# Token factors of a pre-norm applied after the projection, a first norm with its weights as columns, and small parameters loaded inside the feed-forward

## The chip, the cores and the metric

The kernel runs on 1 core of one Trainium2 chip. The metric is the device time of one launch in microseconds. Three runs of the kernel before gave 1834.03, 1839.99 and 1847.09 us, so the median is 1839.99 us.

## The reference, cut to what matters

Ten sublayers work on 256 tokens of 1024 features. Layers 0 and 1 each have a SwiGLU feed-forward (hidden 2816), a mixer (retention and gated delta heads), cross attention to a memory, and a second feed-forward. A last block has another mixer (called mix2 here) and an MLP with squared ReLU (hidden 4096). All values are float32. Each sublayer sits between two RMS norms:

```
h = sublayer(rms_norm(x, w_pre));  x = x + f * rms_norm(h, w_post)     # f = 0.5 or 1
rms_norm(x, w) = x * rsqrt(mean(x*x) + 1e-6) * w
swiglu(u) = (silu(u @ Wg) * (u @ Wu)) @ Wd
mlp(u)    = square(relu(u @ W1)) @ W2
```

The factor rsqrt(mean(x*x) + 1e-6) is one number for each token. It commutes with a projection: (r*u) @ W = r*(u @ W).

## The kernel before, in words

The 256 tokens are two tiles of 128 (t = 0, 1). The residual x stands in SBUF, tokens on partitions. For a projection the normed input u is transposed on PE (L439), 128x128 at a time, into a PSUM tile `tr`, and split into a rounded part and a rest: ACT casts `xh` (L393), DVE subtracts to get `xl` (L394). Each weight arrives as a raw unit of 128x1024 (512 KB) through the SP queue (L410), and is split in the same way into `wh` (ACT, L393) and `wl` (DVE, L394; every second unit of the first mixers' input projection on POOL). A product is then three matmuls (`mm3`, L430): wh with xh, wh with xl, wl with xh. There are 3 raw buffers and 8 pairs of wh and wl; the weights are fetched ahead in the order of their use.

`normT` (L483) is the norm before a sublayer: two squares with sums on ACT (L488), then on POOL an addition (L490), a multiply-add (L453) and a power (L456), then on DVE two `u` (L495), and after each `u` four transposes and the split. `post` (L498) is the norm after it: two squares of the PSUM banks on ACT (L502), the same three steps on POOL (L504, L453, L456), then on DVE `pd` (L510) twice, which needs the factor, and the additions to x (L512). Feed-forward blocks (`ffn`, L600) run over six pieces of the hidden width, j = 0 to 5. In the last piece token tile 0 is finished first, and its `post` and next `normT` run while PE does the down projection of tile 1; then tile 1 follows.

The order of the instructions on every engine comes from the framework's scheduler, which places them by a simulated timeline; engines take them strictly in that order. `gate` (L323) orders a DMA behind the last matmul of a product that was recorded before it (`anchor`), without a wait on the chip. A DMA that is not gated may be placed as early as its buffers allow: small parameters of both layers' mixers (`wab`, `alog`, `dtb`, `lgam`, `gdn_norm`, `conv`, L778 to L789), the `positions` (L662) and mix2's vector of parameters (`pv`, L1291) stand at the start of the SP queue.

Of the kernel before, what the change touches and what calls it, by code (L numbers as in the profile page):

```python
# [108 lines left out]
def pack(inputs):  # L109

    g = {k: np.asarray(v) for k, v in inputs.items()}
    a = {k: g[k] for k in ("norm_pre", "norm_post", "mem_norm", "gdn_norm")}
    a["x"], a["mem"] = g["x"][0], g["mem"][0]
# [156 lines left out]
class K:  # L270
    marks = None

    def __init__(self, ctx, tc, A, out):
# [14 lines left out]
        self.tables, self.used = self.cst.tile([128, 5744], F32, name="tables"), 0  # L288
# [194 lines left out]
    def normT(self, src, wb, T, t):  # L483
# [3 lines left out]
        for g in range(2):  # L487
            nc.scalar.activation(self.junk, src[:, g * 512:g * 512 + 512], AF.Square, accum_out=ss[:, g:g + 1])  # L488
        s1 = self.small(1, "s1")
        nc.gpsimd.tensor_tensor(out=s1, in0=ss[:, 0:1], in1=ss[:, 1:2], op=ALU.add)  # L490
        rs = self.rsqrt(s1, 1.0 / DM, EPS)
        for g in range(2):
            sl = slice(g * 512, g * 512 + 512)
            u = self.w("u")
            nc.vector.scalar_tensor_tensor(out=u, in0=src[:, sl], scalar=rs, in1=wb[:, sl], op0=ALU.mult, op1=ALU.mult)  # L495
            self.toT(u, T, g * 4, 4, t)

    def post(self, t, banks, wb, half):  # L498
        nc = self.nc
        ss = self.small(2, "ss2")  # L500
        for g in range(2):
            nc.scalar.activation(self.junk, banks[g], AF.Square, accum_out=ss[:, g:g + 1])  # L502
        s1 = self.small(1, "s1")
        nc.gpsimd.tensor_tensor(out=s1, in0=ss[:, 0:1], in1=ss[:, 1:2], op=ALU.add)  # L504
        f = 4.0 if half else 1.0
        rs = self.rsqrt(s1, f / DM, f * EPS)
        for g in range(2):
            d = self.w("pd")
            sl = slice(g * 512, g * 512 + 512)
# [90 lines left out]
    def ffn(self, l, s, T, wpost, after):  # L600
# [6 lines left out]
        def act(t, pg, pu, fw):  # L607
# [3 lines left out]
            nc.scalar.activation(s_[:, :fw], pg[:, :fw], AF.Silu)  # L611
# [1416 lines left out]
```

## Time and profile before

| | |
|---|---|
| median of 3 runs | 1839.99 us |
| the profiled execution's own time | 1836.08 us |
| its span | 1834.0 us |
| PE busy | 1768.2 us (96%) |
| DVE, ACT, POOL busy | 1077.6, 908.2, 201.9 us |
| mean granted TensorE clock | 0.975 |
| instructions | 25097 |

The page gives busy time by engine, 40 slices of the span, the DMA queues, the chain that ended last and the costliest groups. In a timeline row the first two numbers are start and duration in us; what stands in square brackets is the idle time of that engine just before the row, and who ended it. "x2" means two instructions merged into a row. A granted clock of 1.00 is 2.4 GHz, 0.50 is 1.2 GHz.

### The profile page before, as it was taken

Reading aid. Unit: us, or ns where it says so; the run is one execution under the profiler, and the core shown is the slowest. Engines: PE = TensorE matmul, PEld = TensorE weight load, DVE = VectorE, ACT = ScalarE, POOL = GpSimd, SP = SyncE. Lnnn points to the kernel's source line nnn. Section 1 sums busy time; section 2 is a strip of 40 time slices with the busy share of each in tenths; the row PEclk is TensorE's granted clock in tenths of the full one; section 3 lists DMA queues with packets and bytes.
Section 4 is the critical chain, followed back from the end, with each engine's and each line's share of the span. In section 5 each row is a group of like instructions: output and inputs, shape, how many; then the busy total and the mean of one; then the engine's idle time right before and its main releaser. Section 6 shows DMA issues by size and latency. Waiting matters only on the chain. (4 is left out here: it accounts for less than half of the span.)

```text
span 1834.0 us, 25097 instructions
## 1 busy us (share of the span) xinstructions
PE 1768.2 (96%) x9712; PEld 1517.9 (83%) x9712; DVE 1077.6 (59%) x1544; ACT 908.2 (50%) x1458; POOL 201.9 (11%) x240
## 2 busy tenths in 40 slices
PE   7999999999999999999999999999999899989998
PEld 6888799888988887888789988988888788878886
DVE  5454577765555546555467676546455668465554
ACT  5434565545544445444465464545344676344442
POOL 0000343121000000000133211000000120110000
PEclk9999999999999999999999999999999999599999
DMA  7555432434536664656544332636567532135552
GB/s 250 207 200 198 155 130 76 132 96 146 162 137 197 197 197 143 207 185 202 187 144 138 96 115 84 206 122 205 164 196 219 170 135 76 39 126 173 187 177 84
DMA packets 82775, 287.05 MB, mean 157 GB/s; under 512 B 11104, under 2 KB 12512, under 8 KB 82656
## 3 DMA queue, kind: packets, MB, share of 16 engines
q1 hardware_dynamic: 82656, 285.46, 47.9%
q8 instruction: 76, 1.25, 0.3%
q14 instruction: 43, 0.35, 0.1%
HBM read 284.37 MB, written 1.05 MB: 156 GB/s over the span
## 5 line engine op out<-in xcount | busy, mean ns | idle before, releaser
L394 DVE TENSOR_TENSOR wl<-raw,wh 128x1024 fp32r<-128x1024 f32 x473 | 576.6, 1231 | 361.3 <-ACT wh L393 323.6
L393 ACT CAST wh<-raw 128x1024 fp32r<-128x1024 f32 x505 | 521.1, 1051 | 339.8 <-DMA raw<-in_wst 196.3
L436 PE MATMUL mm<-wh,xh 128*128 128x512 f32 (+1 forms) x1184 | 457.7, 388 | 6.4 <-ACT xh L393 6.1
L436 PE MATMUL mm<-wh,xl 128*128 128x512 f32 (+1 forms) x1184 | 452.5, 385 | 8.7 <-DVE xl L394 8.6
L436 PE MATMUL mm<-wl,xh 128*128 128x512 f32 (+1 forms) x1184 | 453.1, 384 | 0.3 <-DVE wl L394 0.3
L436 PEld LDWEIGHTS mm<-wh,xl 128*128 128x128 f32 x1184 | 225.2, 191 | 55.0 <-DVE xl L394 12.8
L436 PEld LDWEIGHTS mm<-wh,xh 128*128 128x128 f32 x1184 | 226.0, 191 | 51.2 <-ACT xh L393 10.2
L436 PEld LDWEIGHTS mm<-wl,xh 128*128 128x128 f32 x1184 | 225.7, 191 | 41.3 <-DVE wl L394 1.1
L436 PE MATMUL bank<-wh,xh 128*128 128x512 f32 x544 | 213.3, 392 | 4.4 <-ACT xh L393 4.4
L436 PE MATMUL bank<-wl,xh 128*128 128x512 f32 x544 | 213.8, 393 | 0.0
L436 PE MATMUL bank<-wh,xl 128*128 128x512 f32 x544 | 201.7, 390 | 0.0
L436 PE MATMUL mm<-xh,wh 128*128 128x256 f32 x552 | 160.1, 290 | 0.0
L436 PE MATMUL mm<-xh,wl 128*128 128x256 f32 x552 | 158.5, 288 | 0.7 <-DVE wl L394 0.6
L436 PE MATMUL mm<-xl,wh 128*128 128x256 f32 x552 | 158.7, 288 | 0.0
L394 DVE TENSOR_TENSOR xl<-tr,xh 128x512 fp32r<-128x512 f32 (+1 forms) x118 | 77.2, 664 | 108.0 <-ACT xh L393 107.8
L394 POOL TENSOR_TENSOR wl<-raw,wh 128x1024 fp32r<-128x1024 f32 x32 | 84.7, 2649 | 458.5 <-ACT wh L393 451.9
L393 ACT CAST xh<-tr 128x512 fp32r<-128x512 f32 (+1 forms) x118 | 65.9, 565 | 135.3 <-PE tr L439 134.4
L436 PEld LDWEIGHTS bank<-wh,xh 128*128 128x128 f32 x544 | 102.1, 188 | 28.0 <-ACT xh L393 6.4
L436 PEld LDWEIGHTS bank<-wh,xl 128*128 128x128 f32 x544 | 102.2, 188 | 21.1
L436 PEld LDWEIGHTS bank<-wl,xh 128*128 128x128 f32 x544 | 102.2, 188 | 20.5
L436 PEld LDWEIGHTS mm<-xh,wl 128*128 128x128 f32 x552 | 106.7, 194 | 2.2 <-DVE wl L394 1.5
L436 PEld LDWEIGHTS mm<-xh,wh 128*128 128x128 f32 x552 | 106.9, 194 | 1.4 <-issue 0.7
(458 smaller groups left out, 2004.5 us busy)
## 6 DMA issues: line engine op xcount, KB each, us to landing
raw<-in_wst SPq DMA_DIRECT2D x505, 512.0 KB, 4.4
wpre<-in_norm_pre SPq DMA_DIRECT2D x8, 512.0 KB, 6.5
wpost<-in_norm_post SPq DMA_DIRECT2D x8, 512.0 KB, 6.1
mem<-in_mem SPq DMA_DIRECT2D x4, 512.0 KB, 3.4
rel<-in_rel SPq DMA_DIRECT2D x2, 512.0 KB, 4.4
wmem<-in_mem_norm SPq DMA_DIRECT2D x2, 512.0 KB, 3.8
out<-tables SPq DMA_DIRECT2D x4, 256.0 KB, 2.1
abias<-in_abias SPq DMA_DIRECT2D x3, 256.0 KB, 4.1
```

The lines of the kernel that those rows point to most:

```text
L393: a = self.nc.scalar.copy(h, raw)
L394: return a, (eng or self.nc.vector).tensor_tensor(out=l, in0=raw, in1=h.bitcast(F32), op=ALU.subtract)
L436: return self.place(self.nc.tensor.matmul(out, a, b, start=start, stop=stop))
```

## The change

Three things. (1) Five of the ten pre-norms become "late" (both feed-forwards of both layers, and the MLP; the very first of them in its own form): `u` is x times the weights, without the token factor, and the factor goes into the activation after the projection, as a scale operand of Silu and a factor of the product with `up`, or squared in front of the ReLU. The very first norm transposes x itself, and multiplies by the weights (now a column, `gain0`, 128x8) while it splits; the 512 KB broadcast of that norm's weights is not loaded any more. (2) All norms: the mean's factor goes into the squares' scale, and POOL has two steps in place of three. In `post`, `pd` is bank times weights and needs no factor; the addition to x applies it. (3) The mixer's small parameters are loaded and prepared in piece 3 of the feed-forward before it (`mixer_params`), and `positions`, `madd`, `pv`, `rst` and `lrubd` are gated.

```diff
+    def first_norm(self, T, t, late):
+        for g in range(2):
+            ps = self.tbank()
+            self.transposes(ps, self.x[t][:, g * 512:g * 512 + 512], 4)
+            sl, gn = slice(t * 128, (t + 1) * 128), lambda i: self.gain0[:, g * 4 + i:g * 4 + i + 1]
+            for i in range(4):
+                self.nc.scalar.activation(T[0][g][:, i, sl], ps[:, i * 128:i * 128 + 128], AF.Copy, scale=gn(i))
+            for i in range(4):
+                self.nc.vector.scalar_tensor_tensor(out=T[1][g][:, i, sl], in0=ps[:, i * 128:i * 128 + 128], scalar=gn(i),
+                                                    in1=T[0][g][:, i, sl].bitcast(F32), op0=ALU.mult, op1=ALU.subtract)
+        self.mean_rsqrt([self.x[t][:, g * 512:g * 512 + 512] for g in range(2)], 1.0, late)
...
-    def normT(self, src, wb, T, t):
+    def mean_rsqrt(self, halves, f, out=None, then=None):
         nc = self.nc
         ss = self.small(2, "ss")
         for g in range(2):
-            nc.scalar.activation(self.junk, src[:, g * 512:g * 512 + 512], AF.Square, accum_out=ss[:, g:g + 1])
+            nc.scalar.activation(self.junk, halves[g], AF.Square, scale=math.sqrt(f / DM), accum_out=ss[:, g:g + 1])
+            if then:
+                then(g)
         s1 = self.small(1, "s1")
-        nc.gpsimd.tensor_tensor(out=s1, in0=ss[:, 0:1], in1=ss[:, 1:2], op=ALU.add)
-        rs = self.rsqrt(s1, 1.0 / DM, EPS)
+        nc.gpsimd.tensor_scalar(out=s1, in0=ss[:, 1:2], scalar1=ss[:, 0:1], scalar2=f * EPS, op0=ALU.add, op1=ALU.add)
+        r = self.small(1, "rs") if out is None else out
+        nc.gpsimd.tensor_tensor(out=r, in0=s1, in1=self.mhalf, op=ALU.pow)
+        return r
+
+    def normT(self, src, wb, T, t, late=None):
...
+            if late is None:
+                nc.vector.scalar_tensor_tensor(out=u, in0=halves[g], scalar=rs, in1=w, op0=ALU.mult, op1=ALU.mult)
+            else:
+                nc.vector.tensor_tensor(out=u, in0=halves[g], in1=w, op=ALU.mult)
             self.toT(u, T, g * 4, 4, t)
+        if late is not None:
+            self.mean_rsqrt(halves, 1.0, late)
...
+        def then(g):
+            d = self.w("pd")
+            nc.vector.tensor_tensor(out=d, in0=banks[g], in1=wb[:, g * 512:g * 512 + 512], op=ALU.mult)
+            ds.append(d)
+        rs = self.mean_rsqrt(banks, 4.0 if half else 1.0, None, then)
         for g in range(2):
...
-            nc.vector.scalar_tensor_tensor(out=d, in0=banks[g], scalar=rs, in1=wb[:, sl], op0=ALU.mult, op1=ALU.mult)
-            xg = self.x[t][:, sl]
-            nc.vector.tensor_tensor(out=xg, in0=xg, in1=d, op=ALU.add)
+            xg = self.x[t][:, g * 512:g * 512 + 512]
+            nc.vector.scalar_tensor_tensor(out=xg, in0=ds[g], scalar=rs, in1=xg, op0=ALU.mult, op1=ALU.add)
...
-            nc.scalar.activation(s_[:, :fw], pg[:, :fw], AF.Silu)
+            nc.scalar.activation(s_[:, :fw], pg[:, :fw], AF.Silu, scale=rs[t])
             h = self.w("hf")
-            nc.vector.tensor_tensor(out=h[:, :fw], in0=pu[:, :fw], in1=s_[:, :fw], op=ALU.mult)
+            nc.vector.scalar_tensor_tensor(out=h[:, :fw], in0=pu[:, :fw], scalar=rs[t], in1=s_[:, :fw], op0=ALU.mult, op1=ALU.mult)
...
+            if j == TBJ and s == 1:
+                self.mixer_params(l)
...
+    def mixer_params(self, l):
+        nc, A = self.nc, self.A
+        wab = self.small(128, "wab")
+        self.gate(nc.sync.dma_start(wab, A["wab"][l]))
+        wabh, wabl = self.rtile[:, :128], self.rtile[:, 128:256]
+        self.split(wab, wabh, wabl)
...
+        nc.scalar.activation(nega, par[:, 8:16], AF.Exp)
...
-        nc.sync.dma_start(self.pv, A["pv"])
+        self.gate(nc.sync.dma_start(self.pv, A["pv"]))
...
+                if j == 0:
+                    nc.vector.tensor_tensor(out=r2[t], in0=rs[t], in1=rs[t], op=ALU.mult)
                 r_ = self.w("relu")
-                nc.scalar.activation(r_, ps, AF.Relu)
+                nc.scalar.activation(r_, ps, AF.Relu, scale=r2[t])
...
+        late = lambda l, s: (l, s) == (2, 1) or l < 2 and s in (0, 3)
         self.fetch()
         nc.sync.dma_start(self.x[1], A["x"][128:])
...
-            self.normT(self.x[t], wp, T, t)
+            self.first_norm(T, t, rs[t])
```

How the order moves, at three places. First the SP queue at the start of the program (every row is a DMA; `raw` is a weight unit, `tables` the SBUF tile that holds x, the identity and the small parameters). Before:

```order
L1969 DMA tables<-in_x 128x512 x2
L387 DMA wpre<-in_norm_pre 128x1024
L341 DMA tables<-in_ident 128x128
L410 DMA raw<-in_wst 128x1024
L1974 DMA tables<-in_x 128x1024
L410 DMA raw<-in_wst 128x1024 x2
L662 DMA tables<-in_positions 128x2
L786 DMA tables<-in_gdn_norm 128x1
L778 DMA wab<-in_wab 128x128
L783 DMA tables<-in_alog 128x8
L786 DMA tables<-in_gdn_norm 128x1
L1291 DMA tables<-in_pv 128x33
```

And now:

```order
L2007 DMA tables<-in_x 128x512
L342 DMA tables<-in_ident 128x128
L2010 DMA tables<-in_x 128x512
L342 DMA tables<-in_gain 128x8
L411 DMA raw<-in_wst 128x1024
L2013 DMA tables<-in_x 128x1024
L411 DMA raw<-in_wst 128x1024 x36
L1980 DMA madd_890<-in_madd 128x256
L692 DMA tables<-in_positions 128x2
L342 DMA tables<-in_invf 128x64
L811 DMA tables<-in_gdn_norm 128x1
L803 DMA wab<-in_wab 128x128
```

Before, fourteen small loads stood around the fourth weight unit; now none stands among the first 37 units. In layer 1 six small loads follow one another in the same piece of its feed-forward, and eleven loads in place of eight stand in front of mix2.

Second the ACT queue at the start (`sg` is the Silu of the first gate, the two `xh` after it in the rows of before are those of token tile 1). Before:

```order
L393 CAST wh<-raw 128x1024 x2
L393 CAST rtile<-wab 128x128
L861 ACTIVATE tables<-tables 128x8 x2
L393 CAST wh<-raw 128x1024
L611 ACT_TABLE_LOAD
L611 ACTIVATE sg<-mm 128x256
L393 CAST wh<-raw 128x1024
L393 CAST xh<-tr 128x4x128 x2
```

And now, from the first weight on (`xh` of tile 0's second half, then squares and `xh` of tile 1):

```order
L394 CAST wh<-raw 128x1024
L472 ACTIVATE xh<-tr,tables 128x128 x4
L502 ACTIVATE tables,ss<-tables 128x512
L472 ACTIVATE xh<-tr,tables 128x128 x4
L502 ACTIVATE tables,ss<-tables 128x512
L394 CAST wh<-raw 128x1024 x3
L472 ACTIVATE xh<-tr,tables 128x128 x4
L639 ACT_TABLE_LOAD
L639 ACTIVATE sg<-mm,tables 128x256
```

The last `xh` of tile 1 moved from behind the fifth weight's cast to behind the fourth's. Five activation table loads are new, all of them inside the first feed-forward of layer 0 (three) and of layer 1 (two), around the Exp of `mixer_params` and the sines of the rotary tables.

Third the DVE queue between layer 0's second feed-forward and layer 1's first (a late pre-norm). Before:

```order
L613 TENSOR_TENSOR hf<-mm,sg 128x512
L394 TENSOR_TENSOR wl<-raw,wh 128x1024 x2
L394 TENSOR_TENSOR xl<-tr,xh 128x4x128
L510 SCALAR_TENSOR_TENSOR pd<-bank,rs_6384,wpost 128x512 x2
L512 TENSOR_TENSOR tables<-tables,pd 128x512 x2
L495 SCALAR_TENSOR_TENSOR u<-tables,rs_6403,wpre 128x512 x2
L510 SCALAR_TENSOR_TENSOR pd<-bank,rs_6454,wpost 128x512 x2
L394 TENSOR_TENSOR xl<-tr,xh 128x4x128 x2
L512 TENSOR_TENSOR tables<-tables,pd 128x512 x2
L495 SCALAR_TENSOR_TENSOR u<-tables,rs_6469,wpre 128x512 x2
```

And now:

```order
L641 SCALAR_TENSOR_TENSOR hf<-mm,tables,sg 128x512
L395 TENSOR_TENSOR wl<-raw,wh 128x1024 x2
L535 TENSOR_TENSOR pd<-bank,wpost 128x512 x2
L395 TENSOR_TENSOR xl<-tr,xh 128x4x128
L540 SCALAR_TENSOR_TENSOR tables<-pd,rs,tables 128x512 x2
L523 TENSOR_TENSOR u<-tables,wpre 128x512 x2
L535 TENSOR_TENSOR pd<-bank,wpost 128x512 x2
L395 TENSOR_TENSOR xl<-tr,xh 128x4x128
L540 SCALAR_TENSOR_TENSOR tables<-pd,rs,tables 128x512 x2
L395 TENSOR_TENSOR xl<-tr,xh 128x4x128
L523 TENSOR_TENSOR u<-tables,wpre 128x512 x2
```

`pd` reads no factor any more, the addition to x does (`rs`), and `u` reads none. On PE the transposes of `u` stand where they stood at most boundaries; at the two boundaries from cross attention to the second feed-forward they moved up among the matmuls of the output projection.

## Rows read from the trace of the kernel before

**Rows 1.** Page, part 1: busy us (share) and instructions of each engine.
```profile
PE 1768.2 (96%) x9712; PEld 1517.9 (83%) x9712; DVE 1077.6 (59%) x1544; ACT 908.2 (50%) x1458; POOL 201.9 (11%) x240
```
**Rows 2.** Waits of PE from 30 us on: total us, times, longest.
```profile
PE tr L439 <- DVE u L495: 11.0, 10, 1.9
PE mm L436 <- DVE xl L394: 8.6, 7, 1.6
...
PE mm L436 <- ACT xh L393: 2.6, 5, 1.2
...
PE mm L436 <- DVE wl L394: 0.8, 3, 0.3
```
**Rows 3.** Timeline of the first 24 us: start, duration, engine, instruction.
```profile
9.17 1.05 ACT L393 CAST wh<-raw 128x1024 fp32r<-128x1024 f32 x1 [4.09 <-DMA raw<-in_wst]
...
17.91 1.05 ACT L393 CAST wh<-raw 128x1024 fp32r<-128x1024 f32 x1 [3.21 <-DMA raw<-in_wst]
...
21.88 1.04 ACT L393 CAST wh<-raw 128x1024 fp32r<-128x1024 f32 x1 [1.23 <-DMA raw<-in_wst]
...
23.47 0.39 PE L436 MATMUL mm<-wh,xh 128*128 128x256 f32 x1 [3.52 <-ACT xh L393]
```
**Rows 4.** Timeline of SP: the fourth weight unit is issued.
```profile
13.85 0.43 SPq L410 DMA_DIRECT2D raw<-in_wst  x1
```
**Rows 5.** Stretches: us, busy time by engine, granted clock, DMA share, GB/s.
```profile
101.00:108.00 7.00, 7.00 (x32) 5.78 (x31) 1.79 (x3) 2.99 (x4) 0.00 (x0) 1.00 0.02 6
8.00:10.00 2.00, 1.18 (x6) 1.18 (x7) 1.43 (x3) 0.83 (x1) 0.00 (x0) 1.00 1.02 418
12.00:14.00 2.00, 1.98 (x10) 1.88 (x9) 1.29 (x3) 2.00 (x4) 0.94 (x3) 1.00 0.19 32
```
**Rows 6.** Timeline of PE at the first boundary, feed-forward to mixer.
```profile
207.99 1.38 PE L439 MATMUL tr<-tables,u 128*128 128x128 f32 x8 [0.54 <-DVE u L495]
...
211.65 0.50 PE L436 MATMUL mm<-wh,xl 128*128 128x512 f32 x1 [1.59 <-DVE xl L394]
```
**Rows 7.** Timeline of DVE, ACT and POOL at that boundary.
```profile
203.71 1.28 DVE L512 TENSOR_TENSOR tables<-tables,pd 128x512 f32<-128x512 f32 x2
...
206.32 0.19 POOL L453 TENSOR_SCALAR rs<-s 128x1 f32<-128x1 f32 x1
...
...
207.18 1.42 DVE L495 SCALAR_TENSOR_TENSOR u<-tables,rs,wpre 128x512 f32<-128x512 f32 x2 [2.19 <-POOL rs L456]
...
209.59 1.41 DVE L510 SCALAR_TENSOR_TENSOR pd<-bank,rs,wpost 128x512 f32<-128x512 f32 x2 [1.00 <-POOL rs L456]
...
209.89 2.94 ACT L393 CAST wh<-raw 128x1024 fp32r<-128x1024 f32 x3
...
210.92 1.28 DVE L394 TENSOR_TENSOR xl<-tr,xh 128x512 fp32r<-128x512 f32 x2
```
**Rows 8.** Stretches at half clock behind boundaries, first and last of three, columns as in rows 5.
```profile
212.30:215.70 3.40, 3.40 (x10) 2.62 (x9) 3.40 (x3) 1.25 (x3) 2.04 (x1) 0.50 0.00 0
...
1635.70:1642.50 6.80, 5.64 (x14) 4.17 (x14) 6.62 (x9) 4.28 (x8) 2.24 (x3) 0.50 0.20 54
```
**Rows 9.** Groups by line: form, count, busy us, mean ns, idle before.
```profile
L394 DVE TENSOR_TENSOR wl<-raw,wh 128x1024 fp32r<-128x1024 f32 x473 | 576.6, 1231 | 361.3 <-ACT wh L393 323.6
...
L613 DVE TENSOR_TENSOR hf<-mm,sg 128x512 f32<-128x512 f32 x40 | 27.3, 684 | 13.5 <-PE mm L436 13.5
...
L1143 DVE SCALAR_TENSOR_TENSOR y<-o,rs,zz 128x128 f32<-128x128 f32 x16 | 4.5, 346 | 0.0
```
**Rows 10.** One line, L611: count, duration ns min/median/max, first and last start.
```profile
L611 ACT ACTIVATE sg<-mm x48: 383/592/598, 20.3 to 1411.3; 128x512 f32<-128x512 f32 x40, 128x256 f32<-128x256 f32 x8
...
L611 ACT ACT_TABLE_LOAD x3: 1283/1283/1283, 19.0 to 1242.2; - x3
```
**Rows 11.** DMA issues: KB each, median us from issue to landing.
```profile
raw<-in_wst SPq DMA_DIRECT2D x505, 512.0 KB, 4.4
...
tables<-in_positions SPq DMA_DIRECT2D x1, 1.0 KB, 8.3
```

More of the change, by code (lines that the diff above doesn't have):

```diff
@@ L287, in __init__ @@
         nc = self.nc
-        self.tables, self.used = self.cst.tile([128, 5744], F32, name="tables"), 0
+        self.tables, self.used = self.cst.tile([128, 5776], F32, name="tables"), 0
         self.x = []
@@ L492, in normT @@
+        r = self.small(1, "rs") if out is None else out
+        nc.gpsimd.tensor_tensor(out=r, in0=s1, in1=self.mhalf, op=ALU.pow)
+        return r
+    def normT(self, src, wb, T, t, late=None):
+        nc = self.nc
+        halves = [src[:, g * 512:g * 512 + 512] for g in range(2)]
+        if late is None:
+            rs = self.mean_rsqrt(halves, 1.0)
         for g in range(2):
-            sl = slice(g * 512, g * 512 + 512)
+            w = wb[:, g * 512:g * 512 + 512]
             u = self.w("u")
-            nc.vector.scalar_tensor_tensor(out=u, in0=src[:, sl], scalar=rs, in1=wb[:, sl], op0=ALU.mult, op1=ALU.mult)
+            if late is None:
+                nc.vector.scalar_tensor_tensor(out=u, in0=halves[g], scalar=rs, in1=w, op0=ALU.mult, op1=ALU.mult)
+            else:
+                nc.vector.tensor_tensor(out=u, in0=halves[g], in1=w, op=ALU.mult)
@@ L661, in rotary_tables @@
         pi = self.tab(2).bitcast(I32)
-        nc.sync.dma_start(pi, A["positions"])
+        self.gate(nc.sync.dma_start(pi, A["positions"]))
         pf = self.small(2, "posf")
@@ L768, in mixer_plan @@
         self.plan(("w_out", l), 8)
+    def mixer_params(self, l):
[4 more added lines that the diff above has]
+        self.split(wab, wabh, wabl)
+        par = self.small(24, "par")
+        self.gate(nc.sync.dma_start(par[:, 0:8], self.bc(A["dtb"][l], 8)))
+        self.gate(nc.sync.dma_start(par[:, 8:16], self.bc(A["alog"][l], 8)))
+        self.gate(nc.sync.dma_start(par[:, 16:24], self.bc(A["lgam"][l], 8)))
+        nw = self.small(1, "gdnw")
+        self.gate(nc.sync.dma_start(nw, A["gdn_norm"][l].rearrange("(p o) -> p o", o=1)))
+        nc.vector.tensor_scalar(out=nw, in0=nw, scalar1=0.5, scalar2=None, op0=ALU.mult)
+        cw = self.small(60, "cw")
+        self.gate(nc.sync.dma_start(cw, A["conv"][l]))
+        nega = self.small(8, "nega")
+        nc.scalar.activation(nega, par[:, 8:16], AF.Exp)
+        nc.vector.tensor_scalar(out=nega, in0=nega, scalar1=-1.0, scalar2=None, op0=ALU.mult)
+        self.params = wabh, wabl, par, nw, cw, nega
     def mixer(self, l, T, wpost, after):
@@ L776, in mixer @@
         self.mark("ab")
[L777 to L790 removed]
+        wabh, wabl, par, nw, cw, nega = self.params
         self.st = "m"
@@ L1967, in run @@
         norm = lambda l, s, w: self.bcast(A[two[s, w]] if l == 2 else A["norm_" + w][l, s], "w" + w)
-        for g in range(2):
-            nc.sync.dma_start(self.x[0][:, g * 512:g * 512 + 512], A["x"][:128, g * 512:g * 512 + 512])
         self.anchor = None
+        nc.sync.dma_start(self.x[0][:, :512], A["x"][:128, :512])
         self.ident = self.const("ident", 128)
-        wp = norm(*subs[0], "pre")
+        self.gain0 = self.const("gain0", 8)
+        nc.sync.dma_start(self.x[0][:, 512:], A["x"][:128, 512:])
+        late = lambda l, s: (l, s) == (2, 1) or l < 2 and s in (0, 3)
         self.fetch()
@@ L2005, in run @@
             if l == 2:
-                (self.mix2 if s == 0 else self.mlp)(T, po, after)
+                if s == 0:
+                    self.mix2(T, po, after)
+                else:
+                    self.mlp(T, po, after, rs)
             elif s == 0 or s == 3:
-                self.ffn(l, 1 if s == 0 else 2, T, po, after)
+                self.ffn(l, 1 if s == 0 else 2, T, po, after, rs)
             elif s == 1:
```

47 lines of the change are left out of this document (13 added, 34 removed).

## The prediction, as it was put on record

> **What bounds the kernel now.** I read the page first. PE is busy for 1768.2 of 1834.0 us [rows 1], and no other engine comes near, so a change that adds no matmul can only win where PE stands still or runs at half clock. Then the waits of PE. In the first 24 us PE waits for its first data and then, once, 3.52 us for `xh` [rows 3]. From 30 us on, 11.0 us go to transposes that wait for `u`, ten times, 8.6 us to matmuls that wait for `xl`, 2.6 us to matmuls that wait for `xh`, and 0.8 us to `wl` [rows 2]. The first two lie at the boundaries between sublayers, and the last number says that the weights are in time once the start is over. What is left of PE's idle time belongs to the mixers' own chains, which the change leaves alone.
>
> Then one boundary, where the reader is to see a chain in series. PE stands 0.54 us before `u` and 1.59 us before `xl` [rows 6]. Before the first `u`, DVE adds to x, ACT squares, POOL takes its steps, and DVE has been idle for 2.19 us when the factor comes; the wait for `xl` is a matter of order on DVE: two `pd` of tile 1, which themselves waited 1.00 us for POOL, stand ahead of it from 209.59 us [rows 7]. Last the clock: behind this boundary PE has 3.40 us at a granted clock of 0.50 (1.2 GHz), and behind the last one 6.80 us; the third, between them in time, is like the first [rows 8].
>
> **The start.** Before, the first weight's cast starts at 9.17 us, when its transfer has landed [rows 3]. Now 512 KB less stand ahead of it (the weights' broadcast). At the 418 GB/s that the queue moved then [rows 5] that is 1.25 us, at the three quarters of it that a busy ramp may give 1.7; I take 1.4, so the cast starts at 7.8, ends at 8.85 (1.05 us, [rows 3]), and its `wl` ends at 10.1 (1.231 us of DVE, [rows 9]). That frees the first raw buffer, and the fourth unit is issued at 10.1 in place of 13.85 us [rows 4], because no small load stands ahead of it; DMA moved only 32 GB/s from 12 to 14 us [rows 5], so this was time lost on SP. With the median landing of 4.4 us [rows 11] it lands at 14.5 and not just before 17.91 [rows 3]. On ACT tile 1's last `xh` now stands behind this fourth cast, not behind the fifth, which began at 21.88 [rows 3]. So: cast to 15.5, four scaled copies of 128 columns to 16.7 (0.3 us each is an estimate, a little under the 0.346 us that DVE takes for as many columns, [rows 9]), the four `xl` on DVE at 0.346 us each overlapping to about 17.6. PE then goes on with tile 1 at 17.6 and not at 23.47: **6 us less**. The bounds: if the fourth unit lands as late as it did (17.91), 2.5 us; if the first weight lands as early as the queue's full rate lets it and the copies cost no more than one cast, 8.5.
>
> **The boundaries, waits for `u`.** Of the chain before `u`, each norm and each `post` loses one POOL step, 0.19 us [rows 7] and the gap to the next, by estimate 0.27 together; `post` loses the two additions in series (1.28 us, [rows 7]), since `pd` is made while ACT still squares; and a late `u` needs neither squares nor POOL. Even the shortest gain, at a norm that is not late, is 0.27 + 1.28 + 0.27 = 1.8 us, which is more than most single waits of the ten (11.0 us in all). Three of tile 1 stay in part, where ACT's three weight casts stand ahead of its squares [rows 7] and the norm is not late (both mixers and mix2): I leave 2.0 us. **-9.0 us**; bounds -5 and -11.
>
> **The waits for `xl` and `xh`.** `pd` waits for the bank alone now, and stands done when `xh` comes. What is left is the transposes', ACT's and DVE's own latency: about 0.3 us at four of the boundaries (1.59 at this one), half at the MLP, and tile 1 at mix2 unchanged. Of the 8.6 us [rows 2] I take **-5.5**, and the longest single wait for `xh`, 1.2 us [rows 2], in front of the MLP, where tile 1's `u` was late: **-1.2**. Bounds together -3 and -9.6.
>
> **The clock.** The three stretches cost half their length: (3.4 + 3.4 + 6.8)/2 = 6.8 us [rows 8]. Two other boundaries with waits as long show none, so I do not take the rule that shorter waits bring full clock: half of it, **-3.4**; bounds 0 and -6.8.
>
> **The end.** Nothing covers the last `post`. It loses a POOL step (0.27), and behind the factor DVE has two instructions (1.42 us) where it had two `pd` and two additions (1.41 + 1.28 with a small overlap), all as in [rows 7]: **-1.5**.
>
> **What is added.** `hf` becomes a three-operand instruction: 0.71 us (half of the 1.42 for two, [rows 7]) for 0.684 [rows 9], a few hundredths 48 times, covered by matmuls but at the last piece: **+0.3**. The MLP's two products of one column and the scale operands cost nothing that PE sees. Thirteen small loads (seven and six) and their preparations now stand in piece 3 of two feed-forwards, at 0.43 us of SP each, the length of an issue [rows 4], and three in front of mix2. ACT and DVE wait for them in their order. The cover: the weights there are ahead, for DMA moves 6 GB/s for 7.00 us on end in that piece and PE is busy throughout [rows 5]. When five table loads join ACT's queue there, 1.283 us each [rows 10], they are behind that cover too: the engine mostly waits for PE in a feed-forward. I take 0; bounds 0 and what the fourth rival says.
>
> The sum: -6 - 9.0 - 5.5 - 1.2 - 3.4 - 1.5 + 0.3 = -26.3, from the profiled execution's 1836.1 to **1809.8**. That execution lies 3.9 us below the median of its three runs, 1839.99; of this distance I add half, and forecast **1812 us**. About 1% is what a measurement of this kernel can tell from no change.
>
> **The rivals.**
>
> *A wait takes the place of the one removed* (22%). ACT takes squares, `xh` and three weight casts (2.94 us, [rows 7]) strictly in order; where `u` comes sooner it may only wait longer there. For it: the three boundaries whose norm is not late. Against it: DVE's wait was on POOL, and ACT was idle before most squares. Then half of the 15.7 us comes back, no clock, and 2.5 us of the start: 1836.1 - 7.8 - 2.5 - 1.5 + 0.3 = 1824.6, with the 2 us **1827**.
>
> *Everything goes* (10%): all waits for `u` and `xl`, the clock too, and 8.5 at the start: 11 + 8.6 + 1.2 + 6.8 + 1.5 + 8.5 = 37.6, so 1798.5, with the 2 us **1800**.
>
> *The table loads count* (6%). If ACT's queue has no slack in those pieces, five times 1.283 us is 6.4 us more: **1818**. The Trainium skill (ScalarE: Activation LUTs, What ACT_TABLE_LOAD costs) says that a switch of tables costs the load and a drain, about 2.66 us in all; five such would be 13.3 us and, by that rule, 1825. The rows speak for the load alone: the first load of Silu's table starts at 19.0 us and takes 1.283, and the first Silu starts at 20.3 [rows 10]. I do not expect either on the path, so the chance is small.
>
> *The small loads block* (5%), slower than before. A cast of `wab` on ACT and the preparation of `gdn_norm` on DVE stand among the weights' splits, in order. The longest landing of a small load is 8.3 us [rows 11]. At full price: layer 0's piece 8.3 + three table loads 3.8 + seven issues 3.0 = 15.1, layer 1's 8.3 + 2.6 + 2.6 = 13.5, mix2 8.3, where a column operation on `pv` stands ahead of the first `u`: 36.9 in all. It decides from the point where the weights' lead is gone; each third of it that shows takes back half of the gain. All of it: 1809.8 + 36.9 + 2 = **1849**. Against it stand the 7 us without DMA, and the 0.8 us of waits for `wl` in the whole rest of the run.
>
> My forecast has the other 57%, with 1803 to 1821 as its own range.
>
> **The range** holds 8 of 10: down to **1800** (everything goes), up to **1828** (the first rival); outside it are the fourth rival and the tails. Faster by over 1% (under 1821.6): nearly all of my 57, the 10, half of the 6, and a few of the 22: **0.72**. Within 1%: **0.25**. Slower by over 1%: **0.03**.
>
> **What would show it.** In the changed kernel's profile: PE's third matmul burst (tile 1 of the first gate) near 17.6 us; SP's fourth weight near 10 us; waits of PE for `u` of some 2 us in all and for `xl` of some 3; fewer stretches of 0.50 behind the boundaries; no wait of PE for `wh` or `wl` in piece 3 of the first feed-forwards (near 110 and 820 us). I would be wrong if the waits for `u` come back under the name of `xh`, or if PE waits for weights in piece 3.

## The result and the profile after

The changed kernel took **1819.81 us** (median of four runs, 1817.68 to 1820.98) against 1838.79 before: a ratio of 0.9891, 95% interval 0.9853 to 0.9928. Measured again (last experiment) it took 1824.47 us, ratio 0.9904 (0.9871 to 0.9937). The forecast was 1812 with a range of 1800 to 1828. The direction was right and the size too large: the sum promised 26.3 us for the profiled execution, and the spans show 15.2 (1834.0 to 1818.8). Of the three outcomes, "faster by over 1%" had 0.72; the first measurement lies just inside it (1.09%), the second just outside (0.96%), so that this bet was won by little more than luck.

The page's first part, which answers to [rows 1]: PE is busy for 7 us less, though it does the same 9712 matmuls.

```profile
PE 1760.9 (97%) x9712; PEld 1514.8 (83%) x9712; DVE 1087.6 (60%) x1554; ACT 930.2 (51%) x1475; POOL 205.0 (11%) x196
```

The waits of PE from 30 us on in the changed kernel (total us, times, longest), which answer to [rows 2]:

```profile
PE tr L440 <- DVE u L521: 6.6, 3, 2.5
PE bank L437 <- ACT xh L394: 5.2, 5, 1.5
PE mm L437 <- ACT xh L394: 3.6, 5, 1.2
...
PE mm L437 <- DVE xl L395: 2.5, 5, 1.1
PE P L437 <- DVE P1s L741: 2.5, 3, 1.2
...
PE tr L440 <- DVE hf L641: 2.0, 2, 1.4
...
PE ab L437 <- ACT xh L394: 1.3, 2, 0.8
PE tp L440 <- DVE Y L732: 1.1, 2, 0.6
...
PE tp L440 <- DVE X L746: 0.3, 1, 0.3
```

Two rows of the same view of the kernel before, which the prediction did not need:

```profile
PE bank L436 <- ACT xh L393: 4.4, 5, 0.9
...
PE tp L439 <- DVE X L716: 2.9, 2, 1.9
```

The reader is to see that the ten waits for `u` are three now, that two of these (2.5 and 2.4 us) are longer than any of the ten, and that names stand here (`hf`, `P1s`, `Y`, `ab`) that had no row before. All rows of this view together come to 44.6 us before and to 40.5 after: the waits that the forecast removed came back for the most part under other names. Where the time was won and lost shows when the same matmul is followed through the timelines (start in us; the last two columns are a second profiled execution of the changed kernel, from the last experiment):

| matmul of PE | before | after | ahead | after, second execution | ahead |
|---|---|---|---|---|---|
| a down projection of piece 2, layer 0 | 106.66 | 101.33 | 5.3 | 102.66 | 4.0 |
| last wait of that feed-forward's down projection | 201.69 | 198.91 | 2.8 | 199.45 | 2.2 |
| last wait of layer 0's mixer (output projection) | 404.58 | 404.89 | -0.3 | 406.76 | -2.2 |
| down projection, layer 0's second feed-forward | 715.48 | 709.49 | 6.0 | 711.92 | 3.6 |
| down projection, layer 1's first feed-forward | 908.00 | 900.83 | 7.2 | 903.16 | 4.8 |
| last wait of layer 1's mixer | 1111.36 | 1107.21 | 4.2 | 1113.71 | -2.4 |
| down projection, layer 1's second feed-forward | 1423.03 | 1413.82 | 9.2 | 1419.84 | 3.2 |
| down projection of the MLP's last piece | 1820.58 | 1806.74 | 13.8 | 1817.58 | 3.0 |
| end of the span | 1834.0 | 1818.8 | 15.2 | 1829.7 | 4.3 |

Twice the lead grows, and twice a mixer with its boundary takes some of it back: 3 us each in the first execution, 4.4 and 7.2 in the second. At these boundaries the factor is still in `u`, and tile 1's `u` is late. That boundary in the changed kernel, layer 0, rows of the timelines of DVE, ACT, POOL and PE; they answer to [rows 6, 7]:

```profile
206.52 2.95 ACT L394 CAST wh<-raw 128x1024 fp32r<-128x1024 f32 x3
...
208.60 2.40 POOL L395 TENSOR_TENSOR wl<-raw,wh 128x1024 fp32r<-128x1024 f32 x1 [2.11 <-ACT wh L394]
...
208.92 4.31 DVE L395 TENSOR_TENSOR wl<-raw,wh 128x1024 fp32r<-128x1024 f32 x2
...
209.37 0.63 ACT L502 ACTIVATE tables<-tables 128x512 bf16<-128x512 f32 x1
...
211.10 2.21 POOL L506 TENSOR_SCALAR s<-ss 128x1 f32<-128x1 f32 x1
...
213.99 1.41 DVE L521 SCALAR_TENSOR_TENSOR u<-tables,rs,wpre 128x512 f32<-128x512 f32 x2 [0.76 <-POOL rs L508]
...
214.88 1.94 PE L440 MATMUL tr<-tables,u 128*128 128x128 f32 x8 [2.47 <-DVE u L521]
```

The `xl` that stood behind tile 1's `pd` is gone from the list: PE waits 0.39 us for it now, where it waited 1.59. But ACT takes its three weight casts before the squares of tile 1, DVE two `wl` before its `u`, and POOL's first step needs 2.21 us where it takes 0.30 in most places. PE comes sooner, and waits for 2.47 us where it waited for 1.02 before. The clock falls there, and stays low for twice as long as at this boundary before ([rows 8]); a stretch of the changed kernel, columns as there:

```profile
214.42:221.20 6.78, 5.85 (x25) 4.46 (x26) 2.87 (x5) 2.02 (x3) 2.37 (x1) 0.50 0.57 222
```

### The profile page after: what moved, and what is told of

Same layout as the page of the kernel before. It is cut to its first block, busy times and chain, and to the rows that moved or that the text cites. A ratio compares the mean times of both kernels' runs of the same rounds, so it can differ in the third digit from the quotient of the medians.

```text
span 1818.8 us, 25195 instructions
## 1 busy us (share of the span) xinstructions
PE 1760.9 (97%) x9712; PEld 1514.8 (83%) x9712; DVE 1087.6 (60%) x1554; ACT 930.2 (51%) x1475; POOL 205.0 (11%) x196
## 4 chain that ended last, share of the span: by engine, by line
PE 78%; DVE 8%; DMA 6%; ACT 5%; issue 2%; POOL 1%; SPq 0%; DVEq 0%; ACTq 0%; POOLq 0%
PE mm L437 45%; PE bank L437 20%; DMA raw<-in_wst 5%; DVE wl L395 2%; ACT wh L394 2%; PE tr L440 2%; PE P L437 2%; PE tr L437 1%; PE tp L440 1%; DVE conv L927 1%; PE hs L437 1%; PE oT L437 1%; PE sc L437 1%; ACT tables L502 1%; PE R L437 1%
## 5 line engine op out<-in xcount | busy, mean ns | idle before, releaser
L395 DVE TENSOR_TENSOR wl<-raw,wh 128x1024 fp32r<-128x1024 f32 x473 | 584.0, 1240 | 428.4 <-ACT wh L394 392.3
L395 POOL TENSOR_TENSOR wl<-raw,wh 128x1024 fp32r<-128x1024 f32 x32 | 89.9, 2813 | 476.3 <-ACT wh L394 467.2
L506 POOL TENSOR_SCALAR s<-ss 128x1 f32<-128x1 f32 x44 | 24.3, 552 | 849.1 <-ACT tables L502 849.0
L437 PEld LDWEIGHTS mm<-xl,wh 128*128 128x128 f32 x552 | 107.7, 195 | 0.9 <-issue 0.3
```

Of the source, the lines that this page charges most:

```text
L395: return a, (eng or self.nc.vector).tensor_tensor(out=l, in0=raw, in1=h.bitcast(F32), op=ALU.subtract)
L437: return self.place(self.nc.tensor.matmul(out, a, b, start=start, stop=stop))
L506: nc.gpsimd.tensor_scalar(out=s1, in0=ss[:, 1:2], scalar1=ss[:, 0:1], scalar2=f * EPS, op0=ALU.add, op1=ALU.add)
```

## The experiments

**1 and 2: the parts added one after the other.** The start alone: `first_norm` and the small loads as changed, `normT` and `post` in the text of before. Then the same with the new `post`.

```diff
-        late = lambda l, s: (l, s) == (2, 1) or l < 2 and s in (0, 3)
+        late = lambda l, s: False      # a late factor at the first norm alone
```

> The change's first norm (weights as columns, its factor applied in the first feed-forward) and its small loads inside the feed-forwards; every other norm and every post-norm in the form before. Theory: the start gives the 5.3 us that the changed kernel shows by 100 us, and piece 3 of layer 0's first feed-forward takes back 1.4 (a wait of PE for hf) to 1.9; the waits for u and xl at the boundaries stay as before (11.0 and 8.6 us). Profiled time about 1836.1 - 3.5 = 1832.6. Rival: the wait for hf in piece 3 comes of the factor in hf's own instruction elsewhere or of chance, the loads cost nothing: no wait in piece 3, 1830.8. Second rival: the start's gain is given back at the first boundary: 1836.

> As the one before, and the post-norm in the changed form (pd from the bank alone, two steps on GpSimd, one addition with the factor); the norms in front of the sublayers with their factor in u, as before. Theory: the wait for xl falls from 8.6 to about 3 us, the end of the kernel loses 1.4 us, and the two boundaries in front of cross-attention, which no late factor touches, keep their 2.6 us each; so about two thirds of what the boundaries gained comes from this part: profiled time about 1826. Rival: the late factors carry the gain, and this part alone gives only the end and half of xl: 1831.

Measured: 1839.1 us, ratio 0.9983 (0.9958 to 1.0008), and 1827.3 us, ratio 0.9928 (0.9901 to 0.9956). The start alone gains nothing that can be told: its second rival held. It is 2.3 us ahead at the last down projection of the feed-forward (199.40 against 201.69), and level at the end of layer 0's mixer (404.56 against 404.58), since at that boundary PE waits 4.0 us for `u` in place of 1.6. One expectation failed: the waits for `u` came to 15.4 us in all, not to the 11.0 of before. In front of layer 1's mixer tile 1's `u` starts on DVE at 925.58 us, as before (925.25), but PE waits 2.56 us for it in place of 0.88, because the stretch at half clock that held PE up just ahead of it (918.9 to 922.3 us before) is at full clock here. A wait and a half-clock stretch in front of it stand in for one another, so a longer wait need not be lost time.

The new `post` did what was expected of it: the waits for `xl` fell to 2.3 us, and the time by some 12. The waits for `u` are still 13.4 us with it; the late factors bring them down to 6.6. In time the late factors gave 3 to 8 us, by the two measurements of the changed kernel; the intervals of the ratios overlap, and experiment 12 has an estimate that tells them apart.

**3: weight casts behind tile 1** at the boundaries into both mixers and mix2.

```diff
-FB = ((0, 3), (1, 0), (1, 3))
+FB = ((0, 1), (0, 3), (1, 0), (1, 1), (1, 3), (2, 0))
```

> The changed kernel, with the weight splits in front of both mixers and of mix2 ordered behind tile 1's xh and xl rather than behind tile 0's. Theory: at these three boundaries the three weight casts (2.95 us of ACT) and the wl behind them on DVE and GpSimd are what makes tile 1's u late; without them PE's wait for u falls from 6.6 to under 2.5 us, the stretch at half clock behind it is shorter, and the time is about 5 us less than the changed kernel's: 1815.5 profiled. Rival: the weights become late instead, PE waits for wh or wl inside the mixers, and the time is the same or up to 5 us more. Second rival: u waits for the squares and GpSimd's two steps alone, the wait for u stays above 5 us.

Measured: 1819.5 us, ratio 0.9867 (0.9811 to 0.9922). Of the waits for `u` one of 0.2 us is left, so their cause is shown: the weights' splits ahead of tile 1, that is the casts on ACT together with the `wl` on DVE and GpSimd that were moved with them (experiments 8 and 9 take away parts of them). The time is not lower than the changed kernel's by more than the runs differ. In layer 0's mixer PE waits elsewhere (waits of PE, 205 to 320 us, this kernel):

```profile
PE cum L437 <- DVE tables L861: 2.4, 1, 2.4
PE tp L440 <- DVE Y L732: 1.6, 1, 1.6
PE tp L440 <- DVE X L746: 1.2, 1, 1.2
PE tr L437 <- ACT sqk L937: 1.2, 1, 1.2
```

The weights did become late, though PE does not wait for them by name. ACT waits for raw units (its waits, 214 to 320 us; first the changed kernel, then this one), and what stands behind such a cast on ACT comes later:

```profile
ACT wh L394 <- DMA raw<-in_wst: 4.7, 3, 2.7
```

```profile
ACT wh L394 <- DMA raw<-in_wst: 12.2, 7, 2.9
```

**4: the exponential written back into the mixer.** It was to take one table load out of piece 3 of layer 0, and two out of layer 1's.

```diff
-        nc.scalar.activation(nega, par[:, 8:16], AF.Exp)      # in mixer_params
+        nc.scalar.activation(nega, par[:, 8:16], AF.Exp)      # in mixer, ahead of its first projection
```

> The changed kernel, with the exponential of alog (and its sign) at the mixer's start, as before the change, and no longer in piece 3 of the feed-forward: one table load less in layer 0's piece 3, two less in layer 1's. Theory: in layer 0's piece 3 the 1.28 us of the load stand on ACT among the weight casts, and PE's wait for hf of 1.4 us goes: 1.4 us less, 1819.3 profiled; in layer 1 some tenths. Rival: the landing of the weights behind the small loads on SP's queue sets that wait, and it stays above 1 us: 1820.7.

Measured: 1823.1 us, ratio 0.9898 (0.9847 to 0.9948); PE's wait for `hf` in piece 3 is 1.8 us. But the edit did not do what it was made for: the scheduler placed the exponential in piece 3 all the same, with its table load, and layer 1's two loads stand there too (806.67 and 821.75 us). Timeline of ACT in this kernel:

```profile
104.84 1.28 ACT L896 ACT_TABLE_LOAD   x1
```

So this experiment does not test the theory, and whether table loads make PE wait stays open.

**5: the changed kernel without its start.**

```diff
-            self.first_norm(T, t, rs[t])
+            self.normT(self.x[t], wp, T, t)      # small loads and mixer parameters as before, too
```

> The changed kernel without its start: first norm, broadcast of its weights, small loads and the mixers' preparations as before; late factors and the new post-norm stay. Theory: the start's lead of 3.3 us, as it stands when the first boundary begins (197 against 200 us), is lost by the end of layer 0's mixer, because tile 1's u there does not come sooner by as much and a half-clock stretch falls in another place; so this kernel is as fast as the changed one, profiled 1819 to 1822, and layer 0's mixer ends within 1 us of 398.6. Rival: the lead lasts to the end, and this kernel takes 3.3 us or more longer: 1824 or above.

Measured: 1823.7 us, ratio 0.9904 (0.9870 to 0.9937). Against the changed kernel's first execution the rival looks right: this kernel is 3.4 us behind at the first boundary (202.32 against 198.91) and still 2.7 behind at the end of layer 0's mixer (407.63 against 404.89). Against its second one (199.45 and 406.76) the 2.9 us have become 0.9, and the time is that of the second measurement (1824.5). So these times and profiles alone do not show whether the start's lead lasts; experiment 12 has an estimate.

**6: the mixers' parameters one piece later.**

```diff
-            if j == TBJ and s == 1:
+            if j == TBJ + 1 and s == 1:
```

> The changed kernel, with the mixers' parameters (six small loads and their preparations) one piece later, in piece 4 of the first feed-forwards, apart from the tables that piece 3 loads. Theory: in layer 0 the wait for hf of 1.4 to 2.1 us in piece 3 comes of the small loads and the tables together, since the weights' transfers land late between them; the wait falls under 0.5 us in piece 3 and does not come back in piece 4. What the end gains of that is under 1.4 us, as the mixer takes a lead away. Rival: the loads of the parameters alone delay the weights, and the wait moves to piece 4, with over 1 us. Second rival: the tables alone do it, and it stays in piece 3.

Measured: 1820.9 us, ratio 0.9879 (0.9838 to 0.9919). In the waits of PE before the first boundary `hf` has gone, and piece 4 shows none; first the changed kernel, then this one:

```profile
PE tr L440 <- DVE hf L641: 1.4, 1, 1.4
```

```profile
PE bank L437 <- ACT xh L394: 1.1, 1, 1.1
PE mm L437 <- DVE wl L395: 0.2, 1, 0.2
```

With the six loads ACT's three table loads left piece 3 as well: the changed kernel has them at 106.01, 109.02 and 117.93 us, and this one none between 16.14 and 136.87. In piece 4 the six loads and two table loads (136.87 and 151.88) stand without a wait. So what piece 3 can't carry is the parameters together with the tables; whether by the transfers or by the table loads is open. And it is not the only way to such a wait: experiment 5 has neither the six loads nor a table load in piece 3, and PE waits there too (its waits, 30 to 200 us):

```profile
PE mm L436 <- ACT sg L625: 1.8, 1, 1.8
```

In the time the edit does not show.

**7: a delay in front of the mixer.**

```diff
+        for _ in range(extra):      # 6, in piece 4 of layer 0's first feed-forward
+            self.mm3(ps[:, :fw], *self.lhs(T, 0, t), units[0][0][:, :fw], units[0][1][:, :fw], True, True)
```

> The changed kernel with 18 more matmuls of 512 columns (4.1 us at 0.227 us each) on TensorE in piece 4 of layer 0's first feed-forward; their result is overwritten by the real product behind them. Theory: the mixer behind it is set by ACT, DVE and the weights' transfers as well, so that of the 4.1 us at most 1.5 are left at its end (near 398.6 + 1.5), and the end comes under 1.5 us later. Rival: TensorE's order alone sets the mixer, and all 4.1 us are there at its end: profiled 1824.8.

Measured: 1825.6 us, ratio 0.9906 (0.9871 to 0.9942). The theory fell: the mixer ends at 411.52 us, 6.6 later than in the changed kernel and 4.8 later than in its second profile (406.76). The rival held: the 4.1 us are all there, and more. This mixer did not swallow what came late into it.

**8: no `wl` on GpSimd.**

```diff
-POOLN = 2
+POOLN = 1000
```

> The changed kernel with every second wl of the mixers' input projection on DVE rather than on GpSimd. Theory: at the boundaries into the mixers GpSimd's first step no longer lasts 2.2 us and DVE's first wl no longer 3.2, and tile 1's u comes about 1 us sooner (wait for u 2.5 down to about 1.5); but DVE has 16 times 1.23 us more in each mixer, and since the mixer is set by DVE too, its end comes later by 2 us or more and the time is 3 to 10 us more. Rival: DVE has slack in the mixers; the time is 2 us less.

Measured: 1831.1 us, ratio 0.9951 (0.9924 to 0.9977). Both halves of the theory held in kind. PE's wait for `u` at the first boundary is 1.6 us; the time is 11.3 us above the changed kernel's first measurement and 6.6 above its second, where 3 to 10 were expected. Late in the mixer PE waits for DVE; by these three names the changed kernel waits there for 0.7, 0.5 and 1.4 us (waits of PE, 320 to 412 us, this kernel):

```profile
PE bank L440 <- DVE y L1178: 4.7, 1, 4.7
PE dW L437 <- DVE r L786: 3.1, 2, 2.8
PE KS L437 <- DVE rhs L1145: 2.0, 1, 2.0
```

**9: two casts ahead, not three**, in front of the two mixers; `behind0` is tile 0's `xh` and `xl`, and with `early` 0 no cast stands ahead.

```diff
+        if self.early > 0:
+            self.early, behind = self.early - 1, self.behind0
...
+                    if nl in ((0, 1), (1, 1)):
+                        if t == 0:
+                            self.behind0, self.early = self.put_, 1
+                        else:
+                            self.behind = self.put_
```

> The changed kernel, where at the boundaries into the two mixers two weight casts, not three, stand on ACT ahead of tile 1's squares (none of them in the run that ordered all behind). Theory: what the boundary wins, the weights' loop (raw buffer, transfer, cast, wl) loses: the wait for u goes from 2.4 to 2.5 us each down to about 1.3, ACT waits longer for raw weights behind the boundary than the changed kernel's 4.7 us, and the time stays within 2 us of the changed kernel's 1819.8. Rival: the third cast alone is what matters, the wait falls under 0.7 us, the weights come as before, and the time falls by 3 us or more.

Measured: 1816.5 us, ratio 0.9887 (0.9847 to 0.9928). The wait for `u` in front of layer 0's mixer is 1.5 us, and ACT waits for raw units for 6.6 us from 214 to 320 us, as the theory said. The time is 3.3 us below the first measurement, past the 2 us that the theory allowed, but the four runs spread over 14 us (1810.8 to 1824.9), so a gain is not shown.

**10 and 11: a version that is faster.** No cast ahead in front of the two mixers (mix2 stays as it is), and with it the parameters in piece 4; then the casts alone.

```diff
-                            self.behind0, self.early = self.put_, 1
+                            self.behind0, self.early = self.put_, 0      # 10 and 11
...
+            if j == TBJ + 1 and s == 1:                                  # 10 only
```

> The changed kernel with two of the edits tried before together: the mixers' parameters in piece 4, and in front of the two mixers (not of mix2) the weight casts behind tile 1's xh. Theory: piece 3's wait for hf (1.4 us) goes, the waits for u in front of the mixers (4.8 us) go, of which the weights' loop takes back most in layer 0 and some 2 us in layer 1; 2 to 4 us less than the changed kernel: a median of 1816 to 1818. Rival: stretches at half clock in the mixers fall elsewhere and take all of it back: 1820 or more.

> The changed kernel, where only in front of the two mixers the weight casts stand behind tile 1's xh (mix2 as in the changed kernel, the parameters in piece 3): one of the two edits of the faster version alone. Theory: this edit carries most of that version's gain, since it takes the two waits for u of 2.4 us and the long half-clock stretches behind them; a median within 4 us of that version's 1811.5, and below the changed kernel's in the same call by 4 us or more. Rival: the two edits are needed together, or that version's profile was lucky in its half-clock stretches; 1817 to 1821.

Measured: **1811.5 us** for both edits, ratio 0.9845 (0.9822 to 0.9868), and 1818.1 us for the casts alone, ratio 0.9880 (0.9847 to 0.9913). The first beats the kernel before, and by more than its theory said (1816 to 1818); its interval lies just below that of the changed kernel's second measurement (0.9871 to 0.9937), though not below that of the first. It ends layer 0's mixer at 397.27 us, 7.6 before the changed kernel; of its waits for `u` mix2's is left and one of 0.4 us (waits of PE from 30 us on):

```profile
PE tp L444 <- DVE Y L736: 3.1, 2, 1.6
...
PE tr L444 <- DVE u L525: 2.0, 2, 1.7
...
PE cum L441 <- DVE tables L865: 1.6, 1, 1.6
```

Number 11 lies 6.6 us above it, outside the 4 that the theory gave, and where its rival put it (1817 to 1821). Against the changed kernel beside it (1824.5) it is 6.4 us lower, as the theory's other half said, but the intervals overlap. How much of the 6.6 us is the second edit's and how much the clock's, experiment 12 estimates.

**12: the changed kernel once more.**

> The changed kernel once more, beside the run before it and on its chip. Theory: 1819.8 is what it takes, within 2 us. Rival: the measurements of the kernels lie on several chips and differ by more than that; then only ratios to the kernel before count.

Measured: 1824.5 us (eight runs, 1816.6 to 1833.5), 4.7 above the first time. The theory fell and the rival held: the ratios, 0.9891 and 0.9904, agree within their intervals. Its profiled execution is 10.9 us longer than the first one's (spans 1829.7 and 1818.8). PE stands still for 2.5 us more in it and is busy for 8.4 us more (1769.3 against 1760.9), with the same 9712 matmuls. The mean granted clock differs, one row each, first the first profile:

```profile
core 0: 1818.8 us, clock 0.976
```

```profile
core 0: 1829.7 us, clock 0.970
```

What full speed would have saved is (1 - 0.976) x 1818.8 = 43.7 us in the one and 54.9 in the other: most of the 11 us are the clock's. The waits are not the same in both, either. Their rows from 30 us on come to 40.5 us in the first execution and to 44.3 in the second; there `X` is back at 2.4 us (0.3 in the first, 2.9 before), while `u` (6.8), `xl` (1.7) and `hf` (2.4) are near the first.

Taken off the time, the same sum gives an estimate for every kernel here, since each execution has its time and its mean granted clock on record: time times clock is about what it would have taken at full speed. One execution's figure is good to 0.9 us, by the clock's last digit, and the sum also counts half-clock time in which PE stood still.

| kernel | executions | mean time, us | mean clock | time x clock, mean and its standard error |
|---|---|---|---|---|
| before | 51 | 1841.2 | 0.9717 | 1789.1, 0.4 |
| 1: the start alone | 10 | 1839.1 | 0.9726 | 1788.7, 0.9 |
| 2: start and new `post` | 10 | 1828.0 | 0.9745 | 1781.4, 0.5 |
| changed, both measurements | 12 | 1823.1 | 0.9747 | 1776.9, 0.3 |
| 5: changed without its start | 4 | 1824.1 | 0.9765 | 1781.2, 0.9 |
| 6: parameters in piece 4 | 4 | 1821.0 | 0.9765 | 1778.2, 0.8 |
| 11: casts behind, two mixers | 6 | 1819.0 | 0.9765 | 1776.2, 1.0 |
| 10: as 6 and 11 together | 5 | 1811.4 | 0.9786 | 1772.6, 0.6 |

By this estimate the two measurements of the changed kernel are one (1777.7 and 1776.5), the change gains 12.2 us apart from the clock and some 6 by the clock, and its parts can be told: nothing from the start alone, 7.3 us from the new `post`, 4.5 from the late factors. The start, which is worth nothing with the old norms, is worth 4.3 with the new ones, so experiment 5's rival held after all. Of the 6.6 us between numbers 10 and 11, 3.6 are the second edit's (standard error 1.2) and the rest the clock's, though the same edit alone (number 6) gains nothing.

## Why the prediction was right in kind and too large, by its steps

**The start**: -6 forecast, -5.3 measured at 101 us. The first cast starts at 8.54 us and not at 7.8, since four scaled copies stand ahead of it on ACT, and they wait for the column of weights. But from the fourth weight on the sum came out. SP issues it at 10.87 us (10.1 in the sum), its cast ends at 15.7 (15.5), the four copies behind it at 16.75 (16.7), and the product that waited until 23.47 before, the 38th matmul from the first weight in both kernels, starts at 18.0 (17.6); it is the second of the two in the row at 17.86. Timelines of ACT and PE, changed kernel:

```profile
8.54 1.04 ACT L394 CAST wh<-raw 128x1024 fp32r<-128x1024 f32 x1
...
12.74 2.97 ACT L394 CAST wh<-raw 128x1024 fp32r<-128x1024 f32 x3
15.57 1.18 ACT L472 ACTIVATE xh<-tr,tables 128x128 fp32r<-128x128 f32 x4
...
17.86 0.40 PE L437 MATMUL mm<-wh,xh 128*128 128x256 f32 x2
...
23.87 0.44 PE L440 MATMUL tr<-tables,hf 128*128 128x128 f32 x2 [1.53 <-DVE hf L641]
```

Two things that the sum did not have nearly cancel behind that: the new wait for `hf` takes 1.53 us, and a stretch at half clock that stood there before is gone, which gives 1.7 (a stretch of the kernel before, columns as in rows 5):

```profile
24.60:28.00 3.40, 3.40 (x18) 3.40 (x18) 2.99 (x5) 2.13 (x3) 0.00 (x0) 0.50 1.03 420
```

That they cancel is luck: in the second execution the half-clock stretch is there again (24.2 to 27.6 us), the wait for `hf` is 2.12, and the lead at 101 us is 4.0. Nor does the start's lead last by itself (experiment 1).

**The waits for `u`**: -9.0 forecast, 11.0 to 6.6 and so -4.4 measured. This is the step that failed. Where the factor is late, all are gone, as said. For the three norms that are not late I left 2.0 us; they take 6.6. I had seen the three casts ahead of the squares [rows 7], but counted the wait as if PE came no sooner than before. Experiments 3 and 9 to 11 show that the weights' splits ahead of tile 1 cause it. In front of layer 0's mixer, 2.47 us become 1.6 without GpSimd's `wl` (experiment 8), 1.5 with one cast less (9), and nothing is left with none (3).

This is the first rival, and not at three boundaries only. Of the 15.7 us that `u`, `xl` and `xh` were to give, that rival had half come back; the waits from 30 us on fell by 4.1 us in all (44.6 to 40.5), and by 0.3 in the second execution. The time, 1819.8 and 1824.5, lies between the forecast of 1812 and the rival's 1827.

**The waits for `xl`**: -5.5 forecast, -6.1 measured. Experiment 2 shows that the new `post` does it. **For `xh`**: -1.2 forecast, +1.0 measured (2.6 to 3.6), with 0.8 more in the rows of `bank` and 1.3 in `ab`. The wait in front of the MLP went as forecast, but behind each cross attention a wait of 1.2 us for `xh` stands where 1.5 for `u` stood. So part of what left `u` came back under this name, which the prediction had named as its way to be wrong.

**The clock**: -3.4 forecast. Of the three stretches [rows 8] the first two are twice as long now, and the third is gone (stretches of the changed kernel in front of layer 1's mixer and behind the boundary to the MLP, columns as there), so at these places the clock gave nothing:

```profile
917.50:924.30 6.80, 6.00 (x24) 4.29 (x25) 1.72 (x3) 2.02 (x3) 2.37 (x1) 0.50 0.54 193
1633.00:1643.00 10.00, 9.05 (x41) 7.18 (x41) 7.69 (x10) 5.96 (x8) 0.56 (x1) 1.00 0.75 251
```

By the mean granted clock, 0.975 before and 0.976 after, the profiled executions lost 45.9 and 43.7 us; but a second execution of the changed kernel lost 54.9. Over all executions on record the losses are 52.1 and 46.2 in the mean (experiment 12). So the clock did give some 6 us, but a term of 3.4 us was not to be had from one profile, and not from these three places.

**The end**: -1.5 forecast; from the last down projection to the end 13.4 us became 12.1, so -1.4.

**What is added**: 0 was taken for the small loads. In piece 3 of layer 0 PE waits for 1.4 us (1.6 in the second execution), a tenth of the fourth rival's price for that piece; in layer 1's it does not wait at all. So neither the fourth rival nor the third, with its 6.4 us, comes near its price. The wait goes when the parameters leave the piece (experiment 6); whether their transfers or the table loads that go with them make it is open. In front of mix2 DVE does wait for `pv`, ahead of the first `u`, and PE does not feel it (timeline of DVE):

```profile
1418.27 0.17 DVE L1331 TENSOR_SCALAR tables<-tables 128x7 f32<-128x7 f32 x1 [2.19 <-DMA tables<-in_pv]
```

**What was not seen**: "the mixers' own chains, which the change leaves alone". The change moves the matmuls within the mixers, though it does not touch their text: the scheduler places them anew. The waits of PE from 225 to 400 us, first before, then after:

```profile
PE KS L436 <- DVE rhs L1110: 1.4, 3, 0.7
PE dW L436 <- DVE r L756: 0.5, 1, 0.5
PE QS L436 <- ACT qs L1119: 0.2, 1, 0.2
PE tr L439 <- POOL rr L952: 0.2, 1, 0.2
```

```profile
PE P L437 <- DVE P1s L741: 0.7, 1, 0.7
PE tp L440 <- DVE Y L732: 0.6, 1, 0.6
```

The two rows of after are there, within 0.2 us, in experiment 5, which has the new order of matmuls, and not in experiment 1, which has the old one. Over both mixers these two names came to 3.6 us (2.5 and 1.1), against which 2.6 left `X` in mix2. In the second execution they came to 4.7, and only 0.5 left `X`.

By these steps, of the 11.1 us that are missing 4.6 are tile 1's `u`, 2.2 `xh`, 1.4 piece 3, 1.3 `ab`, 1.2 the clock, 1.0 the new order in the mixers and mix2, 0.8 `bank`, 0.7 the start and 0.1 the end, while `xl` gave 0.6 more than forecast: 12.7, which is 1.6 too many. These are read from two profiles, and they are not independent, since waits and stretches at half clock go together; a second pair would give other shares. What does not hang on one pair is the estimate of experiment 12: without the clock the sum promised 22.9 us, and the change gained 12.2.

## What to carry to other kernels

When one tile's chain is made shorter, look at what stands ahead of the next tile's chain on the engines that work in order: the wait goes there, and PE, which comes sooner, waits longer. An edit that moves an instruction in the program's text may leave it where it was on its engine (experiment 4), so the timeline is the place to see what an experiment did. A change of one norm moves the scheduler's order far from it, so the list of moved instructions is worth reading to its end. And before a few microseconds of clock are counted as a gain, the same kernel's mean granted clock should be seen in more than one execution; time times clock then tells kernels apart that the times alone do not.

## What the runs showed of the hardware

GpSimd's step on 128 single values took 0.30 us in most places and 2.21 us beside two `wl` of DVE in a row (in front of both mixers); one of these `wl`, beside GpSimd's own, took 3.17 us where they take 1.24 in the mean. The group of `wl` on DVE from 208.8 to 213.4 us (count, then ns: least, median, most):

```profile
L395 DVE TENSOR_TENSOR wl<-raw,wh x2: 1212/2192/3172, 208.9 to 212.0; 128x1024 fp32r<-128x1024 f32 x2
```

The Trainium skill (SBUF — State Buffer, Who interferes with whom) states that a DVE instruction with two SBUF inputs contends with a GpSimd instruction that reads SBUF. The trace agrees, and adds that GpSimd's step, which began at 211.10, did not come through between the two: it ended at 213.31, behind the second `wl`, which had begun after it (212.0) and ended at 213.2. The first had ended at 212.1. In experiment 8, where GpSimd has no `wl`, the step began at 209.34 beside three `wl` of DVE in a row and ended at 210.80, just behind the last of them (207.22 to 210.70); rows of its timelines of DVE and POOL:

```profile
207.22 3.48 DVE L395 TENSOR_TENSOR wl<-raw,wh 128x1024 fp32r<-128x1024 f32 x3
...
209.34 1.46 POOL L506 TENSOR_SCALAR s<-ss 128x1 f32<-128x1 f32 x1 [4.24 <-ACT tables L502]
```

The same wait of 1.17 us for `P1s` in layer 1's mixer was followed by 3.40 us at a granted clock of 0.50 in one execution of the changed kernel and by 10.20 us in the other, first the first profile:

```profile
1002.90:1006.30 3.40, 3.40 (x18) 3.40 (x18) 2.91 (x6) 1.70 (x4) 0.00 (x0) 0.50 0.02 5
```

```profile
1003.90:1014.10 10.20, 10.20 (x51) 10.20 (x50) 4.07 (x9) 3.70 (x7) 1.16 (x2) 0.50 0.03 11
```

What decides between the two lengths stays open.
